# Re-ordering waits in a one-core transformer layer: the front, the attention units and the latent scan

## The chip, the cores and the metric

The kernel runs on one core of a Trainium2 chip. A core has TensorE (PE, matrix products, with its weight loads shown as PEld), VectorE (DVE), ScalarE (ACT), GpSimd (POOL) and SyncE (SP), which mostly issues DMAs; the other engines can issue DMAs too. Products land in PSUM banks, everything else lies in SBUF. The metric is the device time of one execution in microseconds (us), as the median of several runs; lower is better.

## The reference, cut to what matters

One layer of a hybrid backbone over 512 latent tokens with 256 context tokens, width 1024, in float32:

```python
mod = silu(c) @ w_ada + b_ada                      # six rows: shift, scale, gate, twice
h  = rms_norm(x, g_norm1) * (1 + sc1) + sh1        # latents;  hc: the same for the context
aq, ak, av, dq, dk, dv, dz, da, db, ga, gd = split_cols(h @ w_in)
q_a = axial_rope(rms_norm(heads(aq))); k_a = axial_rope(rms_norm(heads(ak)))
y_attn = window_ctx_attention(q_a, k_a, v_a, k_ac, v_ac, sink)  # band of 128, context keys, sink
# gated DeltaNet, both directions, chunks of 64; the context scan's state starts the latent scan
u = uv_c - w_c @ S
o = qd_c @ S + intra_c @ u
S = exp(gl_c) * S + kt_c.T @ u
y  = sigmoid(ga) * (y_attn @ w_br_attn) + sigmoid(gd) * (y_d @ w_br_dn)
x1 = x + gt1 * (y @ w_out)
out = x1 + gt2 * (square(relu(hm @ w_mlp1)) @ w_mlp2)
```

There are 8 query heads and 2 key heads of 64 for attention and 8 DeltaNet heads of 64. The context's own outputs are not needed, only its keys, values and final states.

## The kernel before, in words

**Precision and layout.** Activations stand transposed, features on the partitions and the 512 tokens along the free dimension. A large product is three products: each operand is split into a high part (an ACT copy that rounds to the fast float format) and a low part (a DVE subtraction of the two), and high x high, high x low, low x high are added up in one PSUM bank. `split` (L184 to L186) does so for activations; `wload` (L275) fetches a weight tile of 128 x 1024 on SP's queue and makes its high part on ACT (L281) and its low part on DVE (L290) or, for the `late` ones, on ACT and by an adding DMA of POOL (L287, L288).

**Order.** Each engine runs its instructions in order. That order comes from a planner, which goes by the order in the program but pulls forward what its own durations call ready. `tc.add_manual_dep(..., nosync)` ties an instruction behind another one without a semaphore: it only fixes the order. In the front, `pm` chains all PE products in program order.

**Memory.** Most tiles come from one arena of 167 slots of 256 columns (`alloc`), searched from a moving pointer `mem.ptr`; a tile that gets a slot that was freed in the program still waits, on the chip, for the last reader of that slot. Weight tiles rotate through four buffers (tag "wr").

**Front (0 to about 60 us).** For each of eight row groups kt, `strip(kt)` computes the modulation's row from 1 MB of `w_ada` (L218 fetches it, four buffers), `columns(kt)` copies the row out on ACT (L264), turns it into columns with small products, and DVE finishes scale and shift (L270, L271). `latent(kt)` modulates the latents of that group (L356 to L358: DVE, ACT, DVE) and also makes an unsplit copy on ACT (L379), which the gate products `ab_strips` read. `big(kt, tiles)` adds this group's part to the first four DeltaNet key tiles, whose weights `load_early` has split. `warm(kt, n)` issues n products of a matrix of ones. L308, L311 and L319 make the sums of squares, and `context` is the same modulation for the context.

**Attention inputs and matrices (to about 175 us).** `attn_in` computes key, query and value tiles in steps of four products; `k_attn` and `q_attn` normalise (`qk_norm`: the square L499, the product with a block of ones L502, Ln and Exp), rotate and split them. `k_attn` writes the split keys into `KH[kv]` twice, into the rows of the head itself and into the other 64 rows (L536). Woven in are `chunk_mats` (decay and product matrices of the chunks) and, after it, the triangular inversion `invert_all` on DVE (L942, L943), whose inputs are DVE transpositions (`fw` L917, `bw` L921).

**Attention (175 to 290 us).** Eight units (query block, key head). `scores` multiplies queries and keys, takes the maximum on DVE (L600, L601) and the exponential on ACT (L605, through the helper at L149). `outputs` transposes the probabilities on PE (L642), splits them (L185, L186) and multiplies by the values (L632). While unit n is put out, the scores of the next one and some steps of `qts` (the DeltaNet query tiles, L476 and L481, then gate tiles, L1129) are woven in. `weave` always takes the work whose share done is smallest, and on a tie the one that stands first in the list.

**Scans.** `chain_step` is one chunk of one direction in three phases: the products with the state (L1253) and the sum R (L1257, L1258); the products of the inverse with R (L1265), the scaled `uk` (L1271) and ACT copies (L1275, L1277); the new state (L1286, L1302) and the output (L1290, then L1309 in the first half of the latent scan, L1312, L1314, the square L1315 and the sum L1316 in the second). `steps` runs both directions side by side and yields after each phase. Between the phases the program puts `run_fill` (branch and gate products that nothing here waits for, L1174 and L1129) and `run_late` (rows of the remaining modulation: a DMA through the weight buffers, L1193, and a sum on DVE, L1195). Ahead of the latent scan, two groups of query products (`half_products`, L858) are masked into the matrices `IA` on DVE, ACT and POOL (L1381 to L1392), with fill in between (`run_both`).

**Rest (460 to 900 us).** Branch products, output projection, norm and MLP (L351 to L353), which the change leaves alone.

## Time and profile before

| | |
|---|---|
| median of 3 runs | 899.81 us (898.2 to 900.14) |
| the profiled execution's own time | 901.04 us |
| its span, first to last instruction | 899.3 us |
| mean granted TensorE clock | 0.996 |
| PE busy | 876.0 us, 97% of the span |
| DVE busy / ACT busy | 579.0 us / 456.4 us |
| DMA | 107.16 MB, mean 119 GB/s |

How to read it: the span is one execution on the chip, and the time around it (1.7 us) belongs to the run but to no instruction. Busy time of PE is modelled from pipelined matmuls, so a busy PE is not a PE at its peak. A wait is given as "engine line <- engine line that ended it". The granted clock is the share of TensorE's full clock in a stretch. A line of the timeline has the start, the length, the engine, the line, the operation, tiles written <- tiles read, and in brackets the idle time ahead of it with what ended it.

### The profile page before, as it was taken

How to read it: one execution, taken by the hardware profiler on the slowest of the kernel's cores; microseconds unless marked ns; L12 is line 12 of the kernel's file. 1: busy time of each engine (PE TensorE's matmuls, PEld its weight loads, DVE VectorE, ACT ScalarE, POOL GpSimd, SP SyncE). 2: the span in 40 equal slices, each digit the busy share in tenths (PEclk: the TensorE clock that was granted, in tenths of full speed). 3: DMA queues.
4: the chain of work that ended last, by engine and by line, in shares of the span. 5: the costliest groups of instructions: out<-in, count | busy, mean ns of one | idle time of the engine just before them, and what ended most of it. 6: DMA issues, size and time to landing. Idle time of an engine off the chain costs nothing.

```text
span 899.3 us, 16815 instructions
## 1 busy us (share of the span) xinstructions
PE 876.0 (97%) x7070; PEld 705.3 (78%) x7070; DVE 579.0 (64%) x991; ACT 456.4 (51%) x823; POOL 27.6 (3%) x43
## 2 busy tenths in 40 slices
PE   8999999999999999999999999999999999999998
PEld 5678768867777788777778889888888888888886
DVE  4676899878678997678777979831654245334511
ACT  5598756486579886466654345620551134213400
POOL 0010001110000001100000000000000000000000
PEclk9999999999999999999999999999999999999999
DMA  9950445431122233624217873730643224322011
GB/s 353 368 151 27 99 114 120 114 73 36 36 48 48 72 103 113 211 82 141 74 35 243 278 238 92 266 105 1 211 142 99 68 90 141 94 70 92 26 47 47
DMA packets 30892, 107.16 MB, mean 119 GB/s; under 512 B 3808, under 2 KB 4448, under 8 KB 29792
## 3 DMA queue, kind: packets, MB, share of 16 engines
q1 hardware_dynamic: 28368, 97.18, 33.0%
q0 software_dynamic: 2448, 8.91, 5.9%
q8 instruction: 55, 0.90, 0.4%
q14 instruction: 21, 0.17, 0.1%
HBM read 103.98 MB, written 2.10 MB: 118 GB/s over the span
## 4 chain that ended last, share of the span: by engine, by line
PE 77%; DVE 14%; ACT 5%; issue 2%; DMA 2%; SPq 0%; DVEq 0%; ACTq 0%
PE banks L353 15%; PE banks L352 15%; PE banks L351 15%; PE banks L1129 11%; PE banks L206 4%; PE banks L1174 3%; PE banks L476 2%; PE banks L632 2%; PE banks L1265 1%; PE banks L642 1%; DVE m L186 1%; ACT m L149 1%; PE banks L1286 1%; DVE m L943 1%; DVE m L942 1%
## 5 line engine op out<-in xcount | busy, mean ns | idle before, releaser
L352 PE MATMUL banks<-m,m 128*128 128x512 f32 (+1 forms) x536 | 202.3, 380 | 0.0
L353 PE MATMUL banks<-m,m 128*128 128x512 f32 (+1 forms) x536 | 202.3, 380 | 0.0
L351 PE MATMUL banks<-m,m 128*128 128x512 f32 (+1 forms) x536 | 201.9, 380 | 0.3 <-ACT m L357 0.3
L281 ACT ACTIVATE m<-wr 128x1024 fp32r<-128x1024 f32 x68 | 71.6, 1057 | 156.2 <-PE banks L352 78.0
L290 DVE TENSOR_TENSOR m<-wr,m 128x1024 fp32r<-128x1024 f32 x68 | 82.7, 1224 | 67.0 <-PE banks L352 34.2
L351 PEld LDWEIGHTS banks<-m,m 128*128 128x128 f32 x536 | 100.0, 188 | 20.1 <-ACT m L357 0.7
L352 PEld LDWEIGHTS banks<-m,m 128*128 128x128 f32 x536 | 100.3, 188 | 19.3 <-DVE m L358 0.2
L353 PEld LDWEIGHTS banks<-m,m 128*128 128x128 f32 x536 | 100.3, 188 | 18.8
L1574 DVE SCALAR_TENSOR_TENSOR m<-banks,modT,m 128x512 f32<-128x512 f32 x32 | 24.0, 750 | 105.6 <-PE banks L353 105.6
L1129 PE MATMUL banks<-m,wh 128*128 128x512 f32 x320 | 85.6, 405 | 0.0
L281 ACT ACTIVATE wh<-wr 128x1024 fp32r<-128x1024 f32 (+1 forms) x58 | 54.6, 942 | 42.5 <-PE banks L1129 11.1
L476 PE MATMUL banks<-m,wh 128*128 128x512 f32 (+1 forms) x320 | 74.3, 373 | 0.0
L1129 PEld LDWEIGHTS banks<-m,wh 128*128 128x128 f32 x320 | 58.1, 189 | 12.8
L476 PEld LDWEIGHTS banks<-m,wh 128*128 128x128 f32 x320 | 53.1, 189 | 10.3 <-issue 1.7
L185 ACT ACTIVATE m<-m 128x512 fp32r<-128x512 f32 (+1 forms) x56 | 34.9, 628 | 36.0 <-DVE m L1557 19.9
L186 DVE TENSOR_TENSOR m<-m,m 128x512 fp32r<-128x512 f32 (+1 forms) x56 | 38.3, 689 | 20.2 <-ACT m L185 19.8
L206 PE MATMUL banks<-m,m 128*32 128x256 f32 (+3 forms) x352 | 48.3, 373 | 1.1 <-DVE m L358 0.5
L1195 DVE SCALAR_TENSOR_TENSOR m<-wa,m 128x1024 f32<-128x1024 f32 x32 | 38.9, 1221 | 15.2 <-DMA wa<-in_wada 15.1
L290 DVE TENSOR_TENSOR wl<-wr,wh 128x1024 fp32r<-128x1024 f32 (+1 forms) x41 | 41.5, 1013 | 10.6 <-PE banks L1129 7.9
L206 PEld LDWEIGHTS banks<-m,m 128*128 128x128 f32 (+1 forms) x352 | 33.1, 153 | 13.4 <-issue 4.0
L1129 PE MATMUL banks<-m,wl 128*128 128x512 f32 x160 | 43.4, 399 | 0.0
L353 PE MATMUL banks<-m,wl 128*128 128x512 f32 (+1 forms) x120 | 41.7, 349 | 0.6 <-DVE wl L290 0.6
(244 smaller groups left out, 1440.5 us busy)
## 6 DMA issues: line engine op xcount, KB each, us to landing
wr<-in_wm SPq DMA_DIRECT2D x64, 512.0 KB, 3.7
wr<-in_win SPq DMA_DIRECT2D x38, 512.0 KB, 3.6
wa<-in_wada SPq DMA_DIRECT2D x32, 512.0 KB, 4.0
wl<-in_win POOLq DMA_DIRECT2D x17, 512.0 KB, 5.5
m<-in_wada SPq DMA_DIRECT2D x8, 1024.0 KB, 13.9
m<-in_xT SPq DMA_DIRECT2D x8, 512.0 KB, 6.2
wr<-in_wbr SPq DMA_DIRECT2D x16, 256.0 KB, 2.7
wr<-in_wout SPq DMA_DIRECT2D x8, 512.0 KB, 4.4
```

What stands on the lines that cost most here:

```text
L185: A.activation(r32(hi), src, AF.Copy)
L186: return (eng or V).tensor_tensor(r32(lo), src, hi, op=ALU.subtract)
L206: m = PE.matmul(*args, **kw)
L281: h = A.activation(r32(hi), raw, AF.Copy)
L290: V.tensor_tensor(r32(lo), raw, hi, op=ALU.subtract)
L351: mm(acc, w[0][:, k, :], xhi, start=(start and i == 0), stop=False)
L352: mm(acc, w[0][:, k, :], xlo, start=False, stop=False)
L353: mm(acc, w[1][:, k, :], xhi, start=False, stop=(stop and i == n - 1))
L476: PE.matmul(a, w[0][:, k, :], x, start=(k == 0 and x is xs[k][0]), stop=False)
L1129: PE.matmul(acc.ap, w[x][:, k, :], hx[k][y], start=(p == 0), stop=(p == 3 * KT - 1))
L1174: PE.matmul(pa.ap, w[x][:, j, :], r32(Q[y][:, :, j, :]), start=(j == p == 0), stop=(j == 3 and p == 2))
L1195: V.scalar_tensor_tensor(t.ap, wa, 0.5, scr.ap, op0=ALU.mult, op1=ALU.mult, accum_out=modT[:, grp, j:j + 1])
```

## The change

It re-orders, with few instructions removed or added:

- Front: `WARM` goes from 3 and 6 warm-up products to 3 and 3. The high part of each early weight tile is tied behind the row copy of its own number, where only the first was tied before. The unsplit copy L379 leaves `latent` for a new `whole(kt)`, later in the program and tied behind the next row copy. The first early tile's first step stands ahead of strip 2.
- Attention inputs: `k_attn` copies the split keys on ACT into the head's own rows only; two DMAs, issued on ACT's queue, copy them to the other 64 rows of each `KH`. After the inputs of the first inversion, the arena's pointer is set to slot 21.
- Attention: in the list that `weave` gets, the query-tile steps stand ahead of the outputs.
- Latent scan: `behind` ties the late sums and the last additions of the output to the latest R or `uk` of the chain (`mark`). In the second half of the scan the addition, square and sum of a step's output (`add_up`) are put off until after the second phase of the next step. The scan's generator is made earlier, and its first phase runs ahead of the second group of query products; the fill is divided so that as many fill products precede that group as before. `run_late` is called after the second phase of each step, where it was called after the third.

```diff
--- before.py
+++ after.py
@@ -25,7 +25,7 @@
 NHALF = 3
 CTXAT = 3
 CTXS = {3: (), 4: (0,), 5: (1, 2, 3), 6: (4, 5), 7: (6, 7)}
-WARM = 3, 6, 4, 4
+WARM = 3, 3
 NONES = 16
 AHEAD = 2
 LATE = 12
@@ -279,8 +279,8 @@
         else:
             hi, lo = (sb.tile([P, KT, P], F32, tag=t, bufs=NWS, name=nm(t))[:, :n] for t in ("wh", "wl"))
         h = A.activation(r32(hi), raw, AF.Copy)
-        if not early:
-            tc.add_manual_dep(h.ins, row_[0].ins.name, nosync, reason="behind the first row")
+        if len(early) < 4:
+            tc.add_manual_dep(h.ins, row_[len(early)].ins.name, nosync, reason="behind its row")
         if hold:
             tc.add_manual_dep(h.ins, hold[0].ins.name, nosync, reason="behind the latents")
         if late:
@@ -375,9 +375,19 @@
         o = kt * 1024
         hx.append(modulate(t.ap, xt[kt], rx, modA[:, kt, 0:1], modS[:, kt, 0:1],
                            H[:, o:o + 512], H[:, o + 512:o + 1024]))
+        lt[kt] = t
+
+    def whole(kt):
+
+        t = lt.pop(kt)
         h = alloc(512)
-        tx.append((h, A.activation(h.ap, t.ap, AF.Identity, bias=modS[:, kt, 0:1])))
+        m = A.activation(h.ap, t.ap, AF.Identity, bias=modS[:, kt, 0:1])
+        if kt + 1 < KT:
+            tc.add_manual_dep(m.ins, row_[kt + 1].ins.name, nosync, reason="behind the next row")
+        tx.append((h, m))
         t.free()
+
+    lt = {}
 
     def big(kt, *tiles):
 
@@ -390,12 +400,15 @@
     load_early()
     warm(1, WARM[1])
     columns(1)
+    whole(0)
+    big(0, 0)
     strip(2)
     latent(1)
     load_early()
-    big(0, 0, 1)
+    big(0, 1)
     big(1, 0, 1)
     columns(2)
+    whole(1)
     strip(3)
     latent(2)
     load_early()
@@ -403,6 +416,7 @@
     big(1, 2)
     big(2, 0, 1, 2)
     columns(3)
+    whole(2)
     strip(4)
     latent(3)
     load_early()
@@ -411,6 +425,7 @@
     for kt in range(3, KT):
         if kt + 1 < KT:
             columns(kt + 1)
+        whole(kt)
         if kt + 2 < KT:
             strip(kt + 2)
         if kt + 1 < KT:
@@ -532,9 +547,10 @@
         acc.free()
         for src, o in ((t[:, :512], slice(0, 512)), (t2[:, :CTX], slice(512, 768))):
             for kv, r in enumerate(own):
-                for r2 in own:
-                    A.activation(r32(KH[kv][r2, o]), src[r], AF.Copy)
+                A.activation(r32(KH[kv][r, o]), src[r], AF.Copy)
                 V.tensor_tensor(r32(KLo[kv][r, o]), src[r], KH[kv][r, o], op=ALU.subtract)
+        for kv, r in enumerate(own):
+            nc.scalar.dma_start(out=KH[kv][own[1 - kv]], in_=KH[kv][r])
         t.free()
         t2.free()
 
@@ -1054,6 +1070,7 @@
     V.tensor_tensor(X[0][0].ap, X[0][0].ap, xb.ap, op=ALU.add)
     xb.free()
     neg[0].free()
+    mem.ptr = 21
 
     vT = []
 
@@ -1154,7 +1171,7 @@
     ahead = (x for u in units[1:] for x in scores(*u))
     weave((ahead, LEAD))
     for n, u in enumerate(units):
-        work = [(outputs(*u), (span(u[0])[2] + 3) // 2 + 1), (qts, QTS[n]), (inv, INV[3])]
+        work = [(qts, QTS[n]), (outputs(*u), (span(u[0])[2] + 3) // 2 + 1), (inv, INV[3])]
         if n == CO:
             work.append((seq(lambda: list(combine0())), 1))
         weave(*work, (ahead, 4))
@@ -1192,7 +1209,8 @@
             wa = sb.tile([P, KT, P], F32, tag="wr", bufs=NWR, name=nm("wa")).rearrange("p k c -> p (k c)")
             nc.sync.dma_start(out=wa, in_=I["wada2"][grp, j])
             t = alloc(1024)
-            V.scalar_tensor_tensor(t.ap, wa, 0.5, scr.ap, op0=ALU.mult, op1=ALU.mult, accum_out=modT[:, grp, j:j + 1])
+            op = V.scalar_tensor_tensor(t.ap, wa, 0.5, scr.ap, op0=ALU.mult, op1=ALU.mult, accum_out=modT[:, grp, j:j + 1])
+            behind(op)
             t.free()
             if j == 7:
                 V.tensor_tensor(modT[:, grp], modT[:, grp], bada[:, 16 + 8 * grp:24 + 8 * grp], op=ALU.add)
@@ -1255,7 +1273,7 @@
             Rb = alloc(256)
             R = Rb.ap
             V.tensor_tensor(hv(R), hv(z[:, 0:256]), bc(eG[:, d, m4], HD), op=ALU.mult)
-            V.scalar_tensor_tensor(R, vt, -0.5, R, op0=ALU.mult, op1=ALU.add)
+            mark[0] = V.scalar_tensor_tensor(R, vt, -0.5, R, op0=ALU.mult, op1=ALU.add)
         else:
             R = vt
         yield
@@ -1268,7 +1286,7 @@
             Rb.free()
         if not last:
             uk = alloc(256)
-            V.tensor_tensor(hv(uk.ap), hv(u), bc(tb[:, d, m4], HD), op=ALU.mult)
+            mark[0] = V.tensor_tensor(hv(uk.ap), hv(u), bc(tb[:, d, m4], HD), op=ALU.mult)
         if lat:
             us, zqb = alloc(256), alloc(256)
             zq = zqb.ap
@@ -1311,18 +1329,35 @@
             else:
                 V.tensor_tensor(zq, zq, oi[:, :256], op=ALU.add)
                 oi.free()
-                V.tensor_tensor(dst, dst, zq, op=ALU.add)
-                A.activation(zq, dst, AF.Square)
-                V.tensor_reduce(oss[:, cl], hv(zq), axis=AX.X, op=ALU.add)
+                after.append((dst, zqb, cl))
+                return
             zqb.free()
+
+    after, mark = [], [None]
+
+    def behind(op):
+        if mark[0]:
+            tc.add_manual_dep(op.ins, mark[0].ins.name, nosync, reason="behind the chain")
+
+    def add_up():
+
+        while after:
+            dst, b, cl = after.pop(0)
+            behind(V.tensor_tensor(dst, dst, b.ap, op=ALU.add))
+            A.activation(b.ap, dst, AF.Square)
+            V.tensor_reduce(oss[:, cl], hv(b.ap), axis=AX.X, op=ALU.add)
+            b.free()
 
     def steps(r):
         for step in r:
             both = [chain_step(d, step) for d in range(2)]
-            for _ in range(3):
+            for n in range(3):
                 for g in both:
                     next(g, None)
+                if n == 1:
+                    add_up()
                 yield
+        add_up()
 
     def rest():
         for q in range(4):
@@ -1368,11 +1403,15 @@
         b.free()
 
     IA = [alloc(2048, True), alloc(2048, True)]
+    scan = steps(range(NCC, NC_))
     ia = [v64(b.ap) for b in IA]
     for g in range(2):
         ms = slice(16 * g, 16 * g + 16)
         es = slice(512 * g, 512 * g + 512)
-        run_both(FILL[2] - FPAUSE)
+        if g:
+            run_both(FPAUSE)
+            next(scan)
+        run_both(FILL[2] - (1 + g) * FPAUSE)
         qq_ = bank(2)
         qD, qO = diag_off(qq_)
         for _ in half_products(qq_, 1 + g, qT):
@@ -1392,14 +1431,13 @@
             G.memset(ia[1][lo, ms, HC:], 0.0)
     for b in ED + [EO]:
         b.free()
+    ot_ = alloc(2048, True)
     dump("kT0", kT[0].ap)
     dump("qT0", qT[0].ap)
 
-    ot_ = alloc(2048, True)
-    ot = ot_.ap.rearrange("p (c q v) -> p c q v", c=NCL, q=4)
-    for n, _ in enumerate(steps(range(NCC, NC_))):
+    for n, _ in enumerate(scan, 1):
         run_fill(FILL[3][n % 3])
-        if n % 3 == 2:
+        if n % 3 == 1:
             run_late(1)
     for _ in fill:
         pass
```

## The prediction

> **What bounds the kernel now.** I read the page first, then busy time by stage, then what TensorE (PE) waits for, then the moments of those waits. The page's span and engines:
>
> ```profile
> span 899.3 us, 16815 instructions
> ...
> PE 876.0 (97%) x7070; PEld 705.3 (78%) x7070; DVE 579.0 (64%) x991; ACT 456.4 (51%) x823; POOL 27.6 (3%) x43
> ```
>
> PE is the bound: 876.0 of 899.3 us. What removes neither PE work nor PE idle time changes nothing. The stages (stretch; busy time and count of PE, weight loads, DVE, ACT, POOL; granted clock; DMA share; GB/s):
>
> ```profile
> 20.00:34.00 14.00, 13.61 (x98) 9.46 (x98) 8.18 (x15) 7.67 (x13) 0.00 (x0) 1.00 1.02 417
> 34.00:60.00 26.00, 25.69 (x180) 18.45 (x180) 18.20 (x42) 20.16 (x39) 2.47 (x3) 1.00 0.52 182
> ...
> 100.00:175.00 75.00, 71.82 (x598) 57.36 (x597) 72.35 (x145) 40.83 (x61) 6.91 (x8) 1.00 0.54 120
> 175.00:290.00 115.00, 109.25 (x834) 83.49 (x833) 85.16 (x157) 84.65 (x156) 7.25 (x10) 0.99 0.24 51
> ...
> 380.00:460.00 80.00, 76.72 (x1553) 59.32 (x1552) 60.94 (x134) 51.67 (x160) 2.83 (x4) 0.98 0.30 94
> ```
>
> The diff touches just these stages: the front up to 60, attention inputs, attention, latent scan. PE idles 0.4, 0.3, 3.2, 5.8 and 3.3 us in these rows: the stock that a re-ordering can draw on. In the two with most idle time the clock is below 1. The waits of PE (total, times, longest):
>
> ```profile
> PE banks L1265 <- DVE m L1258: 2.8, 3, 1.8
> PE banks L642 <- ACT m L149: 2.6, 2, 2.1
> ...
> PE banks L632 <- DVE m L186: 0.7, 2, 0.4
> ```
>
> and the four longest in the timeline (start, duration, then idle before and releaser):
>
> ```profile
> 102.24 1.13 PE L502 MATMUL banks<-m,c_bones 128*128 128x512 f32 x2 [0.99 <-ACT m L499]
> ...
> 130.44 1.13 PE L502 MATMUL banks<-m,c_bones 128*128 128x512 f32 x2 [1.33 <-ACT m L499]
> ...
> 235.51 1.31 PE L642 MATMUL banks<-c_ident,m 128*128 128x128 f32 x10 [2.07 <-ACT m L149]
> ...
> 392.96 1.15 PE L1265 MATMUL banks<-m,m 64*64 64x64 f32 x32 [1.76 <-DVE m L1258]
> ```
>
> The two longest cost more than their idle time. Windows ahead of and after the third, after the fourth, and around the second:
>
> ```profile
> 233.80:237.20 3.40, 1.62 (x12) 1.37 (x13) 2.95 (x10) 2.96 (x6) 0.86 (x1) 1.00 0.27 24
> 237.20:240.60 3.40, 3.40 (x13) 2.70 (x14) 2.29 (x2) 2.09 (x4) 0.00 (x0) 0.50 0.72 130
> 394.20:397.60 3.40, 3.40 (x68) 2.54 (x69) 1.15 (x4) 1.19 (x4) 0.00 (x0) 0.50 0.00 0
> 128.00:131.40 3.40, 2.07 (x10) 1.19 (x8) 3.37 (x4) 1.18 (x2) 0.00 (x0) 1.00 0.47 155
> ```
>
> After a stretch with PE busy 1.62 of 3.40 us the clock is granted at 0.50 for the next 3.40: up to 1.7 us of PE work lost, and again after the stall at 392.96. After 2.07 of 3.40 (the 1.33 us stall) it is not. So the border lies here between 1.33 and 1.76 us of idle time at a stretch. [...]
>
> **The change, part by part.** Front: three of six warm-up products go, the second tile's first step moves ahead of the third strip, the float copies of the rows (L379) behind the next row, the early weights' copies behind their own rows.
>
> ```profile
> 17.08 1.60 PE L206 MATMUL banks<-ones 128*128 128x128 f32 x12
> ...
> 19.51 0.61 PE L206 MATMUL banks<-c_prm,m 128*128 128x2 f32 x4 [0.82 <-ACT m L264]
> ...
> 19.86 6.32 SPq L218 DMA_DIRECT2D m<-in_wada  x3
> ...
> 34.03 4.06 PE L206 MATMUL banks<-m,m 128*32 128x256 f32 x28
> ```
>
> ```profile
> m<-in_wada SPq DMA_DIRECT2D x1, 1024.0 KB, 14.0
> ```
>
> Half of the 12 warm-up instructions are 0.8 us, and row 1 no longer waits behind a weight copy (0.82 us). But the sixth strip's weights, the first of the three issues at 19.86, land 14.0 us later (the second fence), at 33.9, and that strip starts at 34.03: already on time with its DMA, with a DMA share of 1.02 from 20 to 34. PE can reach the strip earlier only to wait there. The order of issues on SP stays, and an issue freed earlier only joins a full queue. So what is saved ahead of 34 is lost at 34; afterwards 0.3 us of idle time is left. If one of the float copies (0.7 us, like the modulations) delays a modulation, that is +0.7. I take 0, between -0.3 and +0.7.
>
> Attention inputs: of eight ACT copies into KH four go, two DMAs issued on ACT's queue come; `mem.ptr = 21` moves the arena's pointer.
>
> ```profile
> L536 ACT ACTIVATE m<-m x8: 416/520/632, 95.2 to 99.1; 64x512 fp32r<-64x512 f32 x4, 64x256 fp32r<-64x256 f32 x4
> ```
>
> ```profile
> L218 SPq DMA_DIRECT2D m<-in_wada x8: 327/328/647, 3.5 to 25.9; - x8
> ```
>
> ```profile
> 129.79 0.60 ACT L499 ACTIVATE m<-banks 128x512 f32<-128x512 f32 x1 [2.82 <-DVE m L921]
> ```
>
> ACT saves 2 x 0.63 + 2 x 0.42 = 2.1 us and issues twice. No issue on ACT is in the trace; one on SP takes 0.33 to 0.65, so the net is 0.8 to 1.4. The issue also waits for ACT's own copies; queued behind it are the exponentials, a weight copy and the square L499 that PE awaits at 102.24, so the 0.99 can go. The copied halves land before 114 even at the 14.0 us above, and the first scores read them after the last query tile, past 130. At 129.79 the square waits 2.82 us for the transposition L921, which reads the arena slot just freed to it; the moved pointer gives it another, so the 1.33 can go too. But DVE is busy 72.35 of 75 us here and not relieved: what PE does not wait for at L502 it may wait for later, at DVE's convolutions and softmax sums. I take half of 2.3: -1.2; ends -2.3 and +0.6 (issues at 0.65, and another slot just as busy).
>
> Attention: the query-tile step stands ahead of the outputs step, so first at the start of a unit.
>
> ```profile
> 220.91 1.03 ACT L185 ACTIVATE m<-banks 128x1024 fp32r<-128x1024 f32 x1 [0.43 <-PE banks L642]
> ...
> 222.21 0.71 PE L632 MATMUL banks<-m,m 128*128 128x512 f32 x2
> ...
> 240.84 1.08 PE L476 MATMUL banks<-m,wh 128*128 128x512 f32 x4
> ```
>
> At 235.51 the transposes wait for the last exponential of their unit. A query step, four products like the last row's, takes 0.94 us of PE time (0.235 from start to start) and now stands ahead: idle 2.07 becomes 1.13. That is under 1.33, so the clock stays whole: -0.94 - 1.7. The second wait of L642 (2.6 - 2.1 = 0.5) I halve: -0.25. Sum -2.9. In exchange one step less lies between transposes and L632, which now starts 0.3 us after the first half of its input (221.94 against 222.21); other ready products have filled such gaps, so I count 0. Ends: -5.0 (2.07 + 1.7 + 0.5 and the 0.7 of L632), and 0 (0.35, the mean of L632's two waits, in each of 8 units takes back 2.8).
>
> Latent scan: the first state products (64 L1253) and their sums move ahead of the second query group; output sums and late sums stand behind the chain. DVE from 386 to 393 by groups, then rows of the timeline, then a group of the steady scan (428 to 440):
>
> ```profile
> L1388 DVE COPY m<-m 32x512 f32<-32x512 f32 x4 | 1.8, 488 | 0.1
> L1381 DVE TENSOR_TENSOR m<-m,banks 128x512 f32<-128x512 f32 x2 | 1.3, 680 | 0.0
> ...
> L1134 DVE SCALAR_TENSOR_TENSOR m<-m,m 128x512 f32<-128x512 f32 x1 | 0.7, 684 | 0.0
> L1382 DVE TENSOR_TENSOR m<-m,banks 128x512 f32<-128x512 f32 x1 | 0.7, 678 | 0.0
> ```
>
> ```profile
> 386.05 1.10 PE L858 MATMUL banks<-m,m 64*32 64x64 f32 x64
> ...
> 386.21 1.23 DVE L290 TENSOR_TENSOR wl<-wr,wh 128x1024 fp32r<-128x1024 f32 x1 [1.55 <-PE banks L1129]
> ...
> 388.17 3.03 PE L1129 MATMUL banks<-m,wh 128*128 128x512 f32 x12
> ...
> 441.48 1.22 DVE L1195 SCALAR_TENSOR_TENSOR m<-wa,m 128x1024 f32<-128x1024 f32 x1
> ```
>
> ```profile
> L1302 DVE TENSOR_TENSOR m<-m,banks 128x256 f32<-128x256 f32 x3 | 1.3, 419 | 2.9 <-PE banks L1290 2.1 <-PE banks L1286 0.8
> ```
>
> L1265 has its input early, so the wait at 392.96 goes. Late next is the third phase: it needs `uk`, 0.42 us on DVE (as L1302, of its shape), which now stands behind L290 and the four groups, 5.7 us from 386.2 to 391.9, and is ready near 392.3. The same number of fill products precedes, so the weight split L290 and gate sum L1134 fall there again. PE has, from the query products' end at 387.15, L1265 (1.15) and 7 fill products (1.65): done at 390.0, or 390.9 with four pulled forward as now (12 in the row, 8 in the program). It then idles 1.4 to 2.3 us, about today's 1.76, and the halved clock may return. I take 0, ends -3.5 and +0.6. In the steps, two waits of L1265 (2.8 - 1.8 = 1.0) come with output sums and a late sum (441.48) ahead of the chain's sums; tied behind `uk` they fall where DVE idles before L1302 (2.9 us in three): -1.0; if all collide there, 0. The late sums' fetches issue one phase earlier on SP, ahead of later weights; PE has no wait on a weight's DMA among its waits here: 0. The eight fill products left over run behind the scan: 0.
>
> Sum: 0 - 1.2 - 2.9 + 0 - 1.0 = -5.1. The profiled execution took 901.0 us, 1.7 around its span and 1.2 above the median 899.8; so 895.9 for it, 894.7 as a median.
>
> **The rivals.** A: the waits only move. The stall at 235 becomes another behind ACT, and DVE, 96% busy, keeps the attention inputs; only the scan's 1.0 is left: 898.8. The wait that I find behind `uk` speaks for it; against it, that the pointer takes away a real dependence. B: the half clock is not tied to stalls of this size and comes as often: 894.7 + 1.7 = 896.4. Two cases are few, but both follow the longest stalls. [...] C, slower: each of the eight units lacks the moved step ahead of L632. At the full 0.94 that is 7.5 us: 902.2; it decides from 0.86 us a unit. For it: L632 starts 0.3 us after its input. Against: the gaps have been filled with what is ready.
>
> **How the numbers follow.** The measurement can tell this kernel from no change from about 0.2%, 1.8 us. Forecast 0.50, by itself between 891.2 (the scan's -3.5 too) and 897.5; A 0.20; B 0.12; C 0.12; 0.06 for a new 2 us stall with its half clock elsewhere, slower as well. Faster 0.50 + 0.12 = 0.62, same 0.20, slower 0.18. The range goes from 890.5, short of all lower ends together (some 888), to 901.5, and leaves out the slower cases.
>
> **What would show it.** Right: that strip still starts near 34.0; no wait of L499 for L921; L642 waits near 1.1 at that unit with no 0.50 window after it; L1265 without its wait, L1286 with 1.4 to 2.3 us instead. Wrong: the strip before 33.5, more than 1 us of new waits at L632, or a third half-clock window.

## Result and the profile after

The changed kernel takes 904.9 us (median; 904.3 to 906.2) against 899.0 for the kernel before: ratio 1.0066, 95% interval 1.0048 to 1.0083. It is 5.9 us slower, outside the range of 890.5 to 901.5, and the sign is wrong. The diff moves lines by 15 to 38: L642 is L658 in the new profile, L632 is L648, L1265 is L1283, L1286 is L1304, L1129 is L1146, L1195 is L1212, L1463 (the second fetch of x) is L1501, L1473 and L1475 (residual and its square) are L1511 and L1513.

The page of the changed kernel, the same head lines as before:

```profile
span 903.0 us, 16807 instructions
...
PE 876.1 (97%) x7064; PEld 703.6 (78%) x7064; DVE 580.1 (64%) x991; ACT 455.4 (50%) x819; POOL 27.7 (3%) x43
```

PE's busy time is the same to a tenth of a microsecond, so the 3.7 us of span are almost all idle time of PE: 26.9 us against 23.3. By stage (same columns as in the prediction: stretch; busy time and count of PE, weight loads, DVE, ACT, POOL; granted clock; DMA share; GB/s), with 460 to 560 added, first of the changed kernel:

```profile
100.00:175.00 75.00, 73.57 (x612) 58.80 (x611) 72.18 (x145) 40.18 (x61) 6.90 (x8) 1.00 0.54 120
175.00:290.00 115.00, 105.59 (x819) 80.22 (x817) 86.95 (x160) 84.40 (x156) 7.24 (x10) 1.00 0.25 51
...
380.00:460.00 80.00, 78.67 (x1510) 61.05 (x1509) 64.06 (x137) 53.79 (x169) 1.49 (x2) 1.00 0.35 111
460.00:560.00 100.00, 94.19 (x507) 80.38 (x506) 78.91 (x132) 41.24 (x64) 0.00 (x0) 0.98 0.60 199
```

and the last stretch in the kernel before:

```profile
460.00:560.00 100.00, 98.88 (x559) 85.83 (x559) 83.09 (x140) 45.29 (x73) 0.00 (x0) 1.00 0.62 195
```

PE idled 1.1 us there and now idles 5.8, at a clock of 0.98: a stretch that the diff edits nowhere. The moments at which the stages begin, read from the first and last product of a line in the timelines, add up the whole difference:

| stage (PE) | before, us | after, us | difference | predicted |
|---|---|---|---|---|
| start to end of the front (last L206) | 70.1 | 69.3 | -0.8 | 0 |
| to the first scores (L587) | 78.5 | 76.6 | -1.9 | -1.2 |
| attention, to the first L1286 | 148.2 | 151.1 | +2.9 | -2.9 |
| to the norm's transposes (L1426), the latent scan in it | 165.8 | 161.0 | -4.8 | -1.0 |
| to the branch products (first L351) | 13.5 | 14.6 | +1.2 | 0 |
| to the second norm (L1500) | 65.9 | 71.6 | +5.7 | 0 |
| to the last product (L353) | 353.0 | 354.4 | +1.5 | 0 |

The waits of PE in the changed kernel (total, times, longest):

```profile
PE banks L658 <- ACT m L149: 2.6, 5, 0.8
PE banks L351 <- ACT wh L281: 2.5, 1, 2.5
PE banks L319 <- DVE m L311: 2.3, 2, 2.1
PE banks L351 <- ACT m L357: 1.9, 2, 1.0
PE banks L648 <- DVE m L186: 1.7, 3, 0.8
PE banks L1146 <- ACT m L149: 1.6, 2, 1.4
...
PE banks L1304 <- DVE m L1289: 0.7, 1, 0.7
```

The longest of before are gone, 2.8 at L1265 and the single 2.1 at L642, and so are both half-clock windows. The 2.1 at L319 (0.9 before) stands at 8.6 us, in a stage that ends no later for it. In their place stands a wait of 2.5 us in the output projection, and a half-clock window behind it:

```profile
513.00:516.40 3.40, 0.74 (x3) 0.31 (x3) 2.38 (x4) 1.60 (x2) 0.00 (x0) 1.00 0.89 363
516.40:519.80 3.40, 3.40 (x8) 2.72 (x9) 3.33 (x7) 1.06 (x1) 0.00 (x0) 0.50 0.65 188
```

What comes late there is seen on SP's queue (start, duration, instruction, count). Kernel before:

```profile
472.06 1.32 SPq L1463 DMA_DIRECT2D m<-in_xT  x3
478.61 0.42 SPq L1463 DMA_DIRECT2D m<-in_xT  x1
...
506.31 0.33 SPq L248 DMA_DIRECT2D wr<-in_wout  x1
```

Changed kernel:

```profile
502.46 1.81 SPq L1501 DMA_DIRECT2D m<-in_xT  x4
504.38 1.18 SPq L248 DMA_DIRECT2D wr<-in_wout  x1
508.44 8.25 SPq L248 DMA_DIRECT2D wr<-in_wout  x2
```

The four fetches that bring x back for the residual, 2 MB in all, went out at 472 to 479, about when the branch products start (476). Now they go out at 502.5, behind the branch products, ahead of weights for the output projection. Two rows of the DMA view (count, KB, us to landing) price the place in the queue: the weight issued at 506.31 before, and the one at 504.38 after.

```profile
wr<-in_wout SPq DMA_DIRECT2D x1, 512.0 KB, 4.8
```

```profile
wr<-in_wout SPq DMA_DIRECT2D x1, 512.0 KB, 9.5
```

The weight issued at 504.38 lands at 513.9; ACT splits it at 514.02; PE has waited from 512.6 to 515.13.

Why the fetches are late is not in the profile but in the code: the arena. X1, which receives x, is allocated with `keep`, from the top down in the first free 16 units (slots of 256 columns), and its fetch waits for the last reader of what lay there. Following the allocator call by call, X1 gets units 87 to 102 in the kernel before, over the norm's buffers, freed ahead of the branch loop. In the changed kernel it gets units 119 to 134, over branch gates and sums that are freed after that loop. `mem.ptr = 21` alone, or the scan's edits alone, would have put it at units 151 to 166; only the two together put it in the late place.

### The profile page after: what moved, and what is told of

It reads as the page before. It is cut to its first block, busy times and chain, and to the rows that moved or that the text cites. A ratio compares the mean times of both kernels' runs of the same rounds, so it can differ in the third digit from the quotient of the medians.

```text
span 903.0 us, 16807 instructions
## 1 busy us (share of the span) xinstructions
PE 876.1 (97%) x7064; PEld 703.6 (78%) x7064; DVE 580.1 (64%) x991; ACT 455.4 (50%) x819; POOL 27.7 (3%) x43
## 4 chain that ended last, share of the span: by engine, by line
PE 77%; DVE 12%; ACT 6%; DMA 2%; issue 2%; SPq 0%; ACTq 0%; DVEq 0%
PE banks L353 14%; PE banks L351 14%; PE banks L352 14%; PE banks L1146 11%; PE banks L206 5%; PE banks L491 4%; PE banks L1191 3%; PE banks L648 2%; PE banks L1271 1%; ACT m L149 1%; PE banks L1283 1%; DMA m<-in_wada 1%; DVE m L186 1%; PE banks L496 1%; PE banks L1304 1%
## 5 line engine op out<-in xcount | busy, mean ns | idle before, releaser
L351 PE MATMUL banks<-m,m 128*128 128x512 f32 (+1 forms) x536 | 201.9, 380 | 1.9 <-ACT m L357 1.9
L353 PE MATMUL banks<-m,m 128*128 128x512 f32 (+1 forms) x536 | 202.8, 380 | 0.0
L281 ACT ACTIVATE m<-wr 128x1024 fp32r<-128x1024 f32 x68 | 71.6, 1057 | 148.9 <-PE banks L352 76.4
L290 DVE TENSOR_TENSOR m<-wr,m 128x1024 fp32r<-128x1024 f32 x68 | 82.8, 1223 | 63.2 <-PE banks L352 34.2
L351 PEld LDWEIGHTS banks<-m,m 128*128 128x128 f32 x536 | 100.0, 188 | 21.6 <-ACT m L357 2.3
L353 PEld LDWEIGHTS banks<-m,m 128*128 128x128 f32 x536 | 100.6, 188 | 19.2
L1146 PE MATMUL banks<-m,wh 128*128 128x512 f32 x320 | 84.8, 403 | 1.6 <-ACT m L149 1.6
L491 PE MATMUL banks<-m,wh 128*128 128x512 f32 (+1 forms) x320 | 73.2, 371 | 0.0
L1146 PEld LDWEIGHTS banks<-m,wh 128*128 128x128 f32 x320 | 57.5, 188 | 14.7 <-ACT m L149 2.3
L290 DVE TENSOR_TENSOR wl<-wr,wh 128x1024 fp32r<-128x1024 f32 (+1 forms) x41 | 41.5, 1012 | 17.6 <-ACT wh L281 9.8
L206 PE MATMUL banks<-m,m 128*32 128x256 f32 (+3 forms) x352 | 48.4, 373 | 0.6 <-DMA m<-in_wada 0.4
L351 PE MATMUL banks<-m,wh 128*128 128x512 f32 (+1 forms) x120 | 42.5, 356 | 2.5 <-ACT wh L281 2.5
L1212 DVE SCALAR_TENSOR_TENSOR m<-wa,m 128x1024 f32<-128x1024 f32 x32 | 38.8, 1218 | 8.6 <-DMA wa<-in_wada 8.0
L353 PE MATMUL banks<-m,wl 128*128 128x512 f32 (+1 forms) x120 | 42.7, 357 | 1.4 <-DVE wl L290 1.4
L1146 PE MATMUL banks<-m,wl 128*128 128x512 f32 x160 | 43.4, 399 | 0.0
```

Of the source, the lines that this page charges most:

```text
L206: m = PE.matmul(*args, **kw)
L281: h = A.activation(r32(hi), raw, AF.Copy)
L290: V.tensor_tensor(r32(lo), raw, hi, op=ALU.subtract)
L351: mm(acc, w[0][:, k, :], xhi, start=(start and i == 0), stop=False)
L353: mm(acc, w[1][:, k, :], xhi, start=False, stop=(stop and i == n - 1))
L491: PE.matmul(a, w[0][:, k, :], x, start=(k == 0 and x is xs[k][0]), stop=False)
```

## Experiments

Each ratio is against runs of the kernel before on the same chip, whose medians were 898.9, 898.9, 899.9, 899.8 and 899.7 us over the five groups of runs.

### The place of X1

One line ahead of the norm's buffers moves X1:

```diff
+    mem.ptr = 24
     yd = [alloc(1024) for _ in range(4)]
```

> The changed kernel with one line added: the allocator's pointer is set to unit 24 ahead of the norm's buffers, so that X1 (where x is fetched a second time, 2 MB) lies over the end of H, whose last reader is the last gate tile, instead of over the branch sums and gates that are freed after the branch loop. Theory A (the loss after 476 us is the second fetch of x, issued at 502.5 us behind the branch loop instead of at 472.1 us, in the middle of the late sums' and the output's weights): the four fetches go out before 480 us again, the wait of 2.5 us on the output's weights and the half-clock window at 516 us are gone, and the time falls by 5 to 8 us, to 897 to 900. Theory B (the loss comes from the late sums, which this kernel begins one phase later and ties behind the chain): the time stays at 904 to 906.

898.96 us, ratio 0.9993 (0.9982 to 1.0004): 5.9 us (6.6 by the ratios) won back by one line that changes no computation. The fetches go out from 474.7 on, and the stretch reads

```profile
460.00:560.00 100.00, 99.55 (x573) 87.37 (x573) 81.70 (x139) 44.50 (x71) 0.00 (x0) 1.00 0.58 186
```

with no half-clock window. Theory A holds and B falls: the late sums in this kernel begin where they do in the changed one.

The same line with 48:

```diff
+    mem.ptr = 48
```

> The changed kernel with the same line, but the pointer set to unit 48: the norm's buffers move, and X1 still lies over buffers that are freed after the branch loop. Theory A: 904 to 906 us, as without the line, with the fetches of x after 500 us. If the place of the norm's buffers by itself were what matters: as fast as the run with unit 24.

906.39 us, 1.0077 (1.0063 to 1.0091); fetches from 504.6. The line by itself does nothing, the place does.

On the kernel before:

```diff
+    mem.ptr = 72
     yd = [alloc(1024) for _ in range(4)]
```

> The kernel before with the pointer set to unit 72 ahead of the norm's buffers, so that X1 lies over buffers freed after the branch loop. Theory A: the fetches of x go out after 500 us, and the time rises by 4 to 8 us, to 903 to 907. Theory B: no change, 899.

901.35 us, 1.0022 (1.0010 to 1.0034). Slower, but 2.4 us and not 4 to 8. The timeline says why:

```profile
489.28 0.33 SPq L1464 DMA_DIRECT2D m<-in_xT  x1
491.36 1.37 SPq L1464 DMA_DIRECT2D m<-in_xT  x3
```

Unit 72 puts X1 over buffers of which the last is read earlier in the branch loop. Fetches at 472, 489 and 502 cost 0, 2.4 and 5.9 us.

What about the late fetch costs, its bytes or its lateness? Two edits of the changed kernel, with X1 left where it is:

```diff
-        nc.sync.dma_start(out=X1[:, k2 * 1024:(k2 + 1) * 1024], in_=I["xT"][k2])
+        nc.sync.dma_start(out=X1[:, k2 * 1024:k2 * 1024 + 128], in_=I["xT"][k2][:, :128])
+        G.memset(X1[:, k2 * 1024 + 128:(k2 + 1) * 1024], 0.0)
```

> The changed kernel with X1 where it is, freed late, but the four second fetches of x bring only an eighth of their columns (256 KB in place of 2 MB), and GpSimd writes zeros in the rest: the residual's x is left out for seven eighths. Theory A1 (the 2 MB in front of the output's weights cost the time: the weights issued at 504.38 us took 9 us to land): 897 to 900 us. Theory A2 (that X1's space comes free only after the branch loop costs it, whatever is fetched: the residuals wait): 903 to 906.

This kernel leaves out seven eighths of the x that the residual adds. 901.74 us, 1.0019 (1.0006 to 1.0033): between the two ranges, but from branch products to second norm 66.7 us in place of 71.6, where X1 early has 65.1. So about 4.9 of the 6.6 us between the two places go with the bytes (4.2 of 6.6 by the ratios), the half-clock window behind the wait among them (its 12 executions have a mean clock of 0.999 or 1.000, the four of the changed kernel 0.996 to 0.998), and 1.6 with the lateness or what else the place moves. The weight behind the fetches, issued at 505.71, now lands in

```profile
wr<-in_wout SPq DMA_DIRECT2D x1, 512.0 KB, 5.4
```

```diff
-        nc.sync.dma_start(out=X1[:, k2 * 1024:(k2 + 1) * 1024], in_=I["xT"][k2])
+        nc.gpsimd.dma_start(out=X1[:, k2 * 1024:(k2 + 1) * 1024], in_=I["xT"][k2])
```

> The changed kernel with X1 where it is, and the four fetches of x issued from GpSimd's queue in place of SP's: the output's weights stand no longer behind them on SP. If the place in SP's order costs the time: 898 to 901 us. If the bytes in flight do: 903 to 906.

904.35 us, 1.0047 (1.0028 to 1.0065). By time it is the second reading, bytes in flight, but the stage came down from 71.6 to 68.8 us, and the weight issued beside the fetches, at 503.27, lands after

```profile
wr<-in_wout SPq DMA_DIRECT2D x1, 512.0 KB, 7.0
```

in place of 9.5. Leaving SP's queue wins part; with the 2 MB in flight beside it the weight still takes longer than the 3.7 us of the one that `x1_early` issues between 504.5 and 505.5. The last stage of the table stayed at 354.4 to 354.6 us in every changed kernel with X1 late, and is 353.5 in `x1_early`. In it PE waits 1.05 and 0.84 us for the modulated latents (L357), where `x1_early` has one wait of 0.30: ahead of the first of the two, a weight split of DVE (L290, 1.22 us) stands in front of the modulation L356, which it does not in `x1_early`.

### Attention: the order of the list

```diff
-        work = [(qts, QTS[n]), (outputs(*u), (span(u[0])[2] + 3) // 2 + 1), (inv, INV[3])]
+        work = [(outputs(*u), (span(u[0])[2] + 3) // 2 + 1), (qts, QTS[n]), (inv, INV[3])]
```

> The changed kernel with X1 early (unit 24) and the order of the list in attention as before (outputs ahead of the query tiles). Theory C (the query tiles ahead of the outputs cost what attention lost between 150 and 285 us, where the first scores came 2.65 us earlier and the last weighted sum .3 us later): 2 to 3 us faster than the run with X1 early alone. Theory D (the order removed the wait of 2.07 us and its half clock, and the loss comes from elsewhere in attention): 1 to 4 us slower than it.

897.46 us, 0.9981 (0.9971 to 0.9990): 1.5 us faster than X1 early alone, short of C's 2 to 3, and attention is 148.4 us long in place of 151.7. The order costs; D falls as a whole. But its half clock is real: all 12 executions of `x1_early` have a mean clock of 0.999 or 1.000, and with the old order 11 of 12 have 0.997 or 0.998, about 0.002 less, which is what 3.4 us at half clock make in 900. The old order wins although it brings that window back. The same edit the other way round, on the kernel before:

> The kernel before with one edit of the change alone: the query tiles ahead of the outputs in the list of each attention unit. X1 stays at units 87 to 102, where it was. Theory C (the order itself costs, as the 1.5 us say by which the changed kernel with X1 early is slower than the same with the old order): 900.0 to 902 us. Theory D (what the prediction said of the order: the wait of 2.07 us shrinks to 1.13 and the half-clock window goes): 896 to 897.5.

902.40 us, 1.0042 (1.0027 to 1.0058). C again, a little above its numbers. The timeline at the wait that was to shrink:

```profile
235.21 0.98 PE L642 MATMUL banks<-c_ident,m 128*128 128x128 f32 x7 [0.95 <-ACT m L149]
236.76 0.73 PE L632 MATMUL banks<-m,m 128*128 128x512 f32 x2 [0.57 <-ACT m L185]
```

The 2.07 did become 0.95, but 0.57 us come at once at the value products, and the waits of L632 in attention, 0.7 in all before, are now

```profile
PE banks L632 <- DVE m L186: 1.4, 3, 0.7
...
PE banks L632 <- ACT m L185: 0.6, 1, 0.6
```

In which units? `late_start`, below, with the swap in half of them:

```diff
+        if n < 4:
+            work[0], work[1] = work[1], work[0]
```

> The fastest kernel so far (X1 early, old order of the list, first state products behind the second query group; ratio .9965, 896.0 us) with the query tiles first in units 0 to 3 alone. If the cost lies in the units whose value products then wait (in the run with the new order alone these waits of .8 to .94 us stand at 237, 253 and 271 us, in the last units): within .5 us of 896. If every unit pays alike: 897 to 898.

895.78 us, 0.9948 (0.9928 to 0.9967): free, perhaps a gain; the interval overlaps that of the kernel without it. The stall of 2.07 us is gone, or split:

```profile
231.22 0.88 PE L658 MATMUL banks<-c_ident,m 128*128 128x128 f32 x6 [1.02 <-ACT m L149]
...
233.52 0.44 PE L658 MATMUL banks<-c_ident,m 128*128 128x128 f32 x2 [0.75 <-ACT m L149]
```

And with the swap in the other half, `n > 3`:

> The same kernel with the query tiles first in units 4 to 7 alone. If the cost lies in the last units: 897.5 to 899, with the wait of 2.2 us near 235 halved and waits of the value products near 237, 253 and 271 us in its place. If every unit pays alike: 897 to 898. If the first units carry it: 895, since the wait near 235 is halved.

897.92 us, 0.9976 (0.9965 to 0.9988), which overlaps the interval of `late_start`. The stall is still there:

```profile
234.54 2.35 PE L658 MATMUL banks<-c_ident,m 128*128 128x128 f32 x10 [2.07 <-DVE st L626]
```

So the wait for which the order was changed goes by the swap in units 0 to 3. What the swap in units 4 to 7 costs by itself is not shown: PE's waits in attention add up to 6.1 us here and to 6.2 in `late_start`, and the 0.8 us by which attention is longer (149.1 against 148.4) is within what the half clock took here, which this trace has behind the stall and that of `late_start` has not: the ten transposes behind the stall last 2.35 us, in `late_start` 1.31. With all eight swapped, in `x1_early`, the waits are 9.7 us; among them are 0.69, 0.63 and 1.35 us at 252, 270 and 281, of which neither half has any. So the cost comes with the two halves together; why, was not taken apart.

### The latent scan

The whole scan as before, on X1 early with the old order; from the diff these go back:

```diff
-            behind(op)
...
-                after.append((dst, zqb, cl))
...
-                if n == 1:
-                    add_up()
...
-            next(scan)
```

> The changed kernel with X1 early and the old order of the list (897.5 us), and the latent scan as in the kernel before. Theory E (the scan's edits are worth the 4.5 us by which its norm's transposes come earlier, less 1.1 us of gate work that is left behind it): 900 to 901.5. The prediction's sum (1.0 us for the steps, nothing for the start): 898 to 899.

902.53 us, 1.0035 (1.0022 to 1.0049), against 0.9981 with the new scan. In this surrounding the scan's edits are worth about 5 us, more than theory E said, and not the 1.0 of the prediction. Then its parts:

```diff
     def behind(op):
-        if mark[0]:
+        if False:
```

> The changed kernel with X1 early and the old order (897.5 us), without the two ties behind the chain (late sums and output sums); the output sums are still put off by a step, and the first state products still come early. If the ties carry the scan's gain: 899 to 900.5. If they only keep VectorE's order as it would be anyway: 897 to 898.

900.73 us, 1.0020 (1.0010 to 1.0031), against 897.46 with the ties: together they hold over 3 us.

```diff
-    scan = steps(range(NCC, NC_))
...
-        if g:
-            run_both(FPAUSE)
-            next(scan)
-        run_both(FILL[2] - (1 + g) * FPAUSE)
+        run_both(FILL[2] - FPAUSE)
...
-    for n, _ in enumerate(scan, 1):
+    for n, _ in enumerate(steps(range(NCC, NC_))):
         run_fill(FILL[3][n % 3])
-        if n % 3 == 1:
+        if n % 3 == 2:
```

> The changed kernel with X1 early and the old order (897.5 us), with the scan's first state products behind the second query group as in the kernel before, and the late sums at that kernel's phase; ties and deferral stay. If the early start carries the gain (the wait of 1.83 us at the scan's first products and the half clock after it): 899.5 to 901. If the ties carry it: 897 to 898.5.

896.00 us, 0.9965 (0.9953 to 0.9977): the median is 1.5 us lower without the early start, against both expectations. The wait of 1.8 us at the scan's first products of the inverse is back, and it still wins. In the two traces the scan is 0.7 us longer, and the tail shorter, since the eight fill products that an early start leaves over are gone from it: from the norm's transposes to the first branch product 13.4 us in place of 14.6. That is 0.5 of the 1.5 us; the five executions of this kernel also have hardly a half-clock window (mean clock 0.9996, and 0.9978 with the early start).

One tie at a time, on this kernel:

```diff
             op = V.scalar_tensor_tensor(t.ap, wa, 0.5, scr.ap, ...)
-            behind(op)
```

> The same kernel (896.0 us) without the tie of the late sums behind the chain; the output sums keep theirs. The late sums are the longer work on VectorE (two instructions of 1.2 us and .1 us each, one sum per step), so if a tie carries the scan's gain it is this one: 898 to 899.5. Else 896.

902.05 us, 1.0028 (1.0012 to 1.0043): about 5.7 us lost by the ratios, more than expected. The timeline of DVE and PE shows the price of an untied late sum:

```profile
424.17 1.23 DVE L1212 SCALAR_TENSOR_TENSOR m<-wa,m 128x1024 f32<-128x1024 f32 x1 [1.46 <-DMA wa<-in_wada]
425.32 0.08 DVE L1212 DVE_READ_ACCUMULATOR m<-wa,m 128x1 f32 x1
425.32 0.42 DVE L1274 TENSOR_TENSOR m<-banks,eg 128x256 f32<-128x256 f32 x1
```

```profile
426.73 0.68 PE L1282 MATMUL banks<-m,m 64*64 64x64 f32 x16 [0.77 <-DVE m L1275]
428.53 0.68 PE L1282 MATMUL banks<-m,m 64*64 64x64 f32 x16 [1.12 <-DVE m L1275]
```

The sum stands at the head of DVE's queue and waits 1.46 us for its own fetch, with the chain's scaling L1274 behind it, and then runs 1.23 us; PE runs out of fill and waits twice. From 410 to 440 PE is busy 27.68 us at a clock of 0.94; in the kernel with the tie 29.33 at 1.00:

```profile
410.00:440.00 30.00, 27.68 (x539) 20.97 (x538) 21.97 (x46) 16.44 (x59) 0.00 (x0) 0.94 0.41 127
```

```profile
410.00:440.00 30.00, 29.33 (x651) 22.50 (x649) 23.08 (x53) 20.30 (x77) 0.00 (x0) 1.00 0.40 124
```

```diff
-            behind(V.tensor_tensor(dst, dst, b.ap, op=ALU.add))
+            V.tensor_tensor(dst, dst, b.ap, op=ALU.add)
```

> The same kernel without the tie of the output sums behind the chain; the late sums keep theirs. These are instructions of .4 us, behind which the chain waits less: 896 to 897. If the order of the output sums matters as much: 898.

895.33 us, 0.9948 (0.9928 to 0.9968): no loss. Of the two ties, that of the late sums carries the gain. Part of its 5.7 us is the clock: the 12 executions without it have a mean of 0.9951, against 0.9996, some two half-clock windows more. By itself on the kernel before:

```diff
+            op = V.scalar_tensor_tensor(t.ap, wa, 0.5, scr.ap, ...)
+            behind(op)
...
+            mark[0] = V.tensor_tensor(hv(uk.ap), hv(u), bc(tb[:, d, m4], HD), op=ALU.mult)
```

> The kernel before with the tie of the late sums behind the chain alone; X1 stays at units 87 to 102. If the tie carries the scan's gain by itself: 895.5 to 897. If it needs the deferral of the output sums beside it: 898 to 899.5.

897.38 us, 0.9973 (0.9958 to 0.9988): 2.3 us, close to its expected range. In the scan, of the waits of L1265 only the first, 1.8 us, is left. It is not the 5.7 that the tie's removal costs elsewhere: in the kernel before the late sums wait for a fetch only once between 395 and 462, for 0.3 us, and in `late_start` without the tie three times, for 2.6.

### Front and key copies

`late_start` with the front of the kernel before:

```diff
-WARM = 3, 3
+WARM = 3, 6, 4, 4
...
-    big(0, 0)
     strip(2)
...
+        tx.append((h, A.activation(h.ap, t.ap, AF.Identity, bias=modS[:, kt, 0:1])))
```

> The fastest kernel so far (X1 early, old order of the list, first state products behind the second query group; 896.0 us) with the front as in the kernel before. The prediction gave the front nothing and the attention inputs 1.2 us, of which most hung on the front's order: 896 to 897.5. If the front holds the 1.9 us by which front's end to first scores became shorter: 897.5 to 898.5.

896.86 us, 0.9968 (0.9953 to 0.9983).

And with its copies into KH:

```diff
-        for kv, r in enumerate(own):
-            nc.scalar.dma_start(out=KH[kv][own[1 - kv]], in_=KH[kv][r])
+                for r2 in own:
+                    A.activation(r32(KH[kv][r2, o]), src[r], AF.Copy)
```

> The same kernel (896.0 us) with the keys' other halves copied by ScalarE as in the kernel before, in place of the two DMAs. If these copies made the waits of .99 us and 1.33 us in the inputs: 897 to 898.5. If not: 895.5 to 896.5.

897.39 us, 0.9972 (0.9959 to 0.9985). Neither can be told from 0.9965 by time. By the traces, front's end to first scores is 76.7 us in `late_start`, 76.7 with the old front, 77.4 with the old copies, and 78.5 in the kernel before. So the front's edits add nothing, the key DMAs 0.8, and 1.1 remain for what both kernels keep, the moved pointer among it. With the old copies the stall of 0.99 us at L502 is back and that of 1.33 is not: the first hung on the copies, the second on what both keep. The pointer alone was not tried.

### What paid, put together

```diff
+        if n < 4:
+            work[0], work[1] = work[1], work[0]
...
-            behind(V.tensor_tensor(dst, dst, b.ap, op=ALU.add))
+            V.tensor_tensor(dst, dst, b.ap, op=ALU.add)
```

Both on `late_start`.

> X1 early, the front, the key copies and the deferral of the change, the first state products as before, the late sums tied and the output sums not, the query tiles first in units 0 to 3 alone. The two last edits gave 895.8 and 895.3 us each for itself; if they add up: 894 to 895.2. If what they win is the same time twice: 895.2 to 896.

894.37 us, 0.9939 (0.9924 to 0.9955): the fastest of all, 5.3 us under the kernel before, and inside the range for parts that add up; by the ratios it has three quarters of their sum, which the intervals do not tell from the whole.

## Why the prediction was wrong

**The rest, untouched: 0.** This step failed, and it makes the loss: with X1 early the same kernel stands at 0.9993, no change. The prediction looked at what the diff edits after 460 us and found nothing; it took `mem.ptr = 21` for a matter of the attention inputs. But a pointer of an arena is an edit of every allocation behind it. X1 landed on buffers freed 30 us later, and 2 MB went into the queue ahead of weights that PE needed: 5.9 us by time, 7.2 in the last two stages of the traces. No rival had this mechanism; the 0.06 for "a new 2 us stall with its half clock elsewhere" named its effect, without a place or a cause. The place could be worked out beforehand, by following the allocator through the source. That the kernel with X1 early gains nothing, where 5.1 us were forecast, lies with the steps that follow.

**Attention: -2.9, measured +2.9.** The predicted half happened: the wait fell to 0.95 in the run with the order alone (1.13 forecast). What failed is "I count 0" for the step that no longer lies ahead of L632: rival C, as a mechanism. In the changed kernel the value products wait 2.3 us against 0.7, the scores products 1.1 once (L603), the gate and query tiles' products 1.6 (L1146, 1.4 of it at once). C's price, 0.86 us a unit in all eight, was wrong: with the order in units 0 to 3 alone the waits of PE in attention add up to 7.1 us, against 6.2 in `late_start`, and no time is lost. That C's time, 902.2, is near the 902.4 of the order alone is an accident.

**The half clock: -1.7.** The step tied it to the length of the stall, and took it for sure. What the traces show in its place is the PE work in stretches of 3.413 us, counted off from the first rise of the clock: a clock of 0.50 followed 13 of them, with 0.48 to 1.65 us of work, and none with more (last section). `late_start` has the old order and the old stall, from 232.43 to 234.50:

```profile
234.50 1.31 PE L658 MATMUL banks<-c_ident,m 128*128 128x128 f32 x10 [2.07 <-ACT m L149]
```

In this execution one stretch ends and the next begins at 233.51, within the stall; they keep 2.32 and 2.36 us of work, and the clock stays whole:

```profile
230.10:233.51 3.41, 2.32 (x16) 1.52 (x13) 3.23 (x6) 1.99 (x3) 0.00 (x0) 1.00 0.00 0
233.51:236.93 3.42, 2.36 (x17) 1.85 (x17) 2.97 (x8) 2.98 (x8) 0.86 (x1) 1.00 0.52 62
```

In the profiled execution of before, 1.72 of its 2.07 us fell into one stretch, from 233.79, which was left with 1.62 us of work, and the clock behind it was 0.50. So the border between 1.33 and 1.76 us of idle time was read from three cases that do not carry it. An estimate from these counts and the trace of before: if the row of stretches may begin anywhere, about six of ten places leave one over this stall with less than 1.65 us of work, so the 1.7 was worth about 1.0. That much the order did win, since the executions of `x1_early` have a mean clock of 0.999 or 1.000, but its new waits took more. Rival B was right that the length of a stall does not decide, and wrong that the half clock comes as often.

**The scan: 0 at the start and -1.0 in the steps, measured -4.8 up to the norm and +1.2 behind it.** The steps came as forecast: the two waits of L1265 there, 1.0 us, are gone. The start was priced too low: the wait at L1304 that was to replace that of L1265 is 0.7 us, not 1.4 to 2.3, no half clock followed, and the window at 394, up to 1.7 us, is gone. "The eight fill products left over run behind the scan: 0" failed the other way: 1.2 us moved from the scan to the tail, where they have nothing to cover. So the early start, for all that it won in this pair of traces, is not shown to be a gain: without it the median is about 1.4 us lower by the ratios (0.9981 and 0.9965, whose intervals just overlap). The words "they fall where DVE idles" priced the late sums at their own duration. That fits the kernel before, where the tie alone wins 2.3 us and the sums wait 0.3 us for their fetches between 395 and 462. Among the other edits an untied sum also holds the queue until its fetch has landed (2.6 us in three waits), and there the tie is worth more than twice as much.

**The front and the attention inputs** came near. The sixth strip starts at 33.73 (34.03 before; wrong would have been before 33.5). Front's end lies between 69.1 and 70.3 us in the kernels with the new front, at 69.6 in the mean, and between 69.9 and 70.3 in those with the old one, at 70.0 in the mean: -0.4, just outside -0.3 to +0.7, and -0.8 in this pair. The inputs gained 1.9 (range -2.3 to +0.6). L499, now L514, waits for the transposition L921 no longer; both old stalls of L502 are gone and one of 0.58 us came, at 111.29.

**The base.** The profiled execution of before held two half-clock windows. The prediction priced the end of one and the return of the other as if every execution had both. Most have fewer: 66 of 115 have a mean clock of 0.998 or above (last section).

## What to carry to other kernels

An edit of an arena's pointer, or of the order of its allocations, changes every later allocation: list what each big buffer that a DMA fills lies over, before and after, and when that was last read. A sum that nobody waits for still holds up what stands behind it on its engine while its own fetch is under way (1.46 us in `late_tie_off`), so tie it behind the work that is waited for. Fill that is saved early in a chain is no gain if it then runs where nothing needs cover. Where a wait is removed by moving work ahead of it, look for the product that had that work in front of it. Where a stall's half clock is part of a forecast, price it with a chance.

## What the runs showed of the hardware

The mean granted clock of an execution comes mostly in steps of 0.002, which is what one half-clock window of 3.4 us makes in 900: the trace of before has 0.996 and two such windows, that of the changed kernel 0.998 and one. Over 115 executions of the kernel before, 20 had a mean clock of 1.000 and a mean span of 896.2 us, 45 had 0.998 and 897.5, 33 had 0.996 and 899.0, and 6 had 0.994 and 901.7; the rest lie between. By these steps, an estimate for the executions without a trace, the same program got none, one, two or three windows, with spans 1.3, 1.5 and 2.6 us apart, and with two the profiled execution was at the slow end of its own kernel (901.0 against a median of 899.8 in the three runs then known).

The clock records of the 20 traces, one of each kernel, show where the windows lie. The granted clock changes 46 times after its first rise to 1.00, each time at a whole multiple of 3.413 us from that rise, to within 3 ns. The first rise comes 4.0 to 6.9 us after the start of the span (5.09 in the trace of before, 4.37 in that of the changed kernel), so the same stall lies at another place of these stretches from one trace to the next. The 20 traces have 5197 of these stretches that end ahead of the last product, and 13 of them are followed by a clock of 0.50: these held 0.48 to 1.65 us of PE work, and none of the others held less than 1.65. In the trace of before the two are those from 233.79, with 1.62 us of work, and from 390.80, with 1.65; the next least of its 260 stretches, from 127.97, held 2.08 and kept the clock at 1.00. These are counts of this kernel's traces, and no run varied the work in a stretch by itself. The stall of 2.07 us had a half-clock window behind it in the trace of before and none in that of `late_start`: to a forecast such a stall is a chance of one, not a sure one.
